# Six of the eight neighbourhood-attention gate units of an encoder layer, computed as three pairs with seven block products each

## The chip, the cores and the metric

The kernel runs on one core of one Trainium2 chip. The core has five engines that work through their own queues in order and wait for one another by semaphores: PE (TensorE, the matmul engine; its weight loads are listed apart as PEld), DVE (VectorE), ACT (ScalarE), POOL (GpSimd) and SP (SyncE), which here only issues transfers. Sixteen DMA engines carry out the transfers. The metric is the time of one execution in microseconds (us), the median of several runs; lower is better. Beside it there is one profiled execution, which is the source of all durations.

## The reference, cut to what matters

The layer takes 512 tokens of width 1024. It projects them to queries, keys, values and gate logits for three attention branches, merges the gated branches, normalises, and ends with 16 expert feed-forward blocks that pick their tokens.

```python
z = jnp.einsum('bsd,df->bsf', x, w_in[l])
q_na, k_na, v_na, q_g, k_g, v_g, q_m, gate_logits = jnp.split(z, _split_points(), axis=-1)
y_na  = neighbourhood_attention(...)      # branch 0
y_gqa = gqa_attention(...)                # branch 1
y_mem = memory_attention(...)             # branch 2
branches = jnp.stack([y_na, y_gqa, y_mem], axis=2)
proj = jnp.einsum('bsgk,gkd->bsgd', branches, w_branch[l])
gates = jax.nn.sigmoid(gate_logits + b_gate[l]).reshape(B, S, N_BRANCH, D)
merged = jnp.sum(gates * proj, axis=2)
mix = jnp.einsum('bsd,de->bse', merged, w_out[l])
x = layer_norm(DN_ALPHA * x + mix, ln1_g[l], ln1_b[l])
ffn = expert_choice_ffn(x, w_router[l], w_gate_up[l], w_down[l])   # 16 experts
x = layer_norm(DN_ALPHA * x + ffn, ln2_g[l], ln2_b[l])
```

The change is in the gate logits of branch 0: for each of eight groups of 128 gate columns, a product of a 1024 x 128 piece of the weights with the 512 tokens, then the sigmoid, which the kernel writes as a tanh of half the argument.

## The kernel before, in words

**Units.** The dense weights arrive as 74 units of 128 x 1024 numbers (512 KB each), in the order in which PE uses them. Units 34 to 53 belong to the neighbourhood queries and keys and to branch 1; 54 to 61 are the eight gate units of branch 0; 62 to 65 are its projections (two projection products each, `pr0` to `pr7`); 66 to 73 are the output projection (`wo`, `woc`). `Stream` handles them: `_dma` (L162) issues a unit's transfer on SP into one of two halves of the tile `raw_twin` (the first units go to wide tiles), `_split` (L176) turns a unit into a rounded high part (a copy on ACT, L100) and a low part (a subtraction on DVE, L101), `take` hands it out and `prefetch` keeps splits and transfers two units ahead. A unit's transfer can be issued only when the unit two before it in `raw_twin` has been split. The split parts live in three homes that rotate.

**Products.** Each product is done three times, high by high, high by low and low by high, into the same PSUM bank (`t_piece`, L281, matmuls at L284 to L286). A gate unit is thus 8 x 3 = 24 matmuls of 128 x 128 weights with 512 columns. The tokens are `xh` and `xl`. A run of 256-column matmuls of the same kind stands in `n_chunk` (L307 and its neighbours, tile `gq`).

**Order.** The program's order on each engine is the order written out in the code. `run` (L805) walks through a stage; at each `yield` it takes a step of the attention pipeline (`at.step()`) and one piece of background work from the list `bg`. Branch 1 (`g_branch(1)`) has 22 yields, six in each of its first three rounds; the gate stage of branch 0 (`g_na_gates`, L568) has one per unit. After it comes `g_na_proj` (L964), which for each projection product multiplies by the gate (L973), adds the merged sum (L974) and splits the result for the output projection (L979, L986), all of it on DVE and ACT. The router's weight scaling, its sums on PE (`wps`, L935) and its centring (L938, L939) are background pieces in the gate stage. PSUM has eight banks: three rotate under the name `mm`, two each under `S` and `T`, one under `Y`.

**Expert blocks.** 201 MB of expert weights come in blocks of 1 or 2 MB (`w<-in_wx`, issued at L843). `RING` lists the tiles (Q1 to Q7, raw, Q9, VS, G1, M) in the order in which blocks go to them; each of these tiles has an earlier use, and a block waits until that is over. `ring.more(n)` loads the next block if fewer than n are in. It is hooked into the issue of units 60, 62, 64 and 66 (the list `after`), then 71 and 73; `ring.upto(9)` follows in the output projection. The rest waits for Q9, which holds the split parts of the last output-projection units, and from there on the blocks stream.

**Tiles that the change touches.** Q4 holds the query parts of branch 1, then twice the position bias `bm` of even head pairs, then the gates `sg`. Q1 holds the neighbourhood queries and keys, Q2 the output of branch 1, Q6 its keys, Q7 the attention's probabilities (`att_twin`), VS the shifted values. From the last attention step on, Q1, Q2, Q5, Q6, Q7 and VS have no use but the ring's.

Of the kernel before, what the change touches and what calls it, by code (L numbers as in the profile page):

```python
# [9 lines left out]
F32 = mybir.dt.float32  # L10
# [8 lines left out]
P = 128  # L19
# [53 lines left out]
def layer_kernel(ctx: ExitStack, tc: tile.TileContext, xt, xn, first0, wu, bgate, rpb, gains, wrt,  # L73
# [14 lines left out]
    def R(tag, shape, name, dt=F32, bufs=None):  # L88
        return rp.tile(shape, dt, name=name, tag=tag, bufs=bufs)
# [3 lines left out]
    def PB(tag, name, shape=(P, 512)):  # L93
        return ps.tile(list(shape), F32, name=name, tag=tag, bufs=PS_BUFS[tag])
# [4 lines left out]
    def hi_lo(hi, lo, src):  # L99
        nc.scalar.copy(hi, src)  # L100
        nc.vector.tensor_tensor(lo, src, hi.bitcast(F32), op=ALU.subtract)  # L101
# [398 lines left out]
    def gate_piece(g, j, dst):  # L500
        u, = ws.take()
        ws.prefetch()
        acc = PB("mm", f"gate{g}{j}")
        t_unit(acc, u, xh, xl)
        return lambda: nc.scalar.activation(dst, acc, AF.Tanh, bias=bg_t[:, g * 8 + j:g * 8 + j + 1], scale=0.5)
# [8 lines left out]
    def g_branch(g, first, pre=None):  # L514
        if first:
            ST["macc"] = R("M", [P, KD, S], "macc")
        macc = ST["macc"]
        for jp in range(4):
            th = []
            for jj in range(2):  # L520
                t = R("t", [P, S], f"th{g}{jp}{jj}", bufs=2)
                th.append(t)
                ev = gate_piece(g, 2 * jp + jj, t)
                yield
                ev()
            u, = ws.take()
            ws.prefetch()
            for jj in range(2):
                j = 2 * jp + jj
                acc = proj_piece(u, jj, *ST[f"y{g}"], f"pr{g}{j}")  # L530
                yield
                if first:
                    nc.vector.scalar_tensor_tensor(macc[:, j], th[jj], 1.0, acc, op0=ALU.add, op1=ALU.mult)
                else:
                    tmp = R("tmp", [P, S], f"tm{g}{j}", bufs=2)
                    nc.vector.scalar_tensor_tensor(tmp, th[jj], 1.0, acc, op0=ALU.add, op1=ALU.mult)
                    nc.gpsimd.tensor_tensor(macc[:, j], macc[:, j], tmp, op=ALU.add)
            if pre:
                yield from pre(jp)

    def g_na_qk(hp):
# [4 lines left out]
        for i in range(2):  # L546
# [5 lines left out]
            for h in range(2):  # L552
# [8 lines left out]
                else:  # L561
# [3 lines left out]
                    for o in (hb, lb):  # L565
                        nc.vector.tensor_tensor(klo[o:o + 64, h], src, k[o:o + 64].bitcast(F32), op=ALU.subtract)

    def g_na_gates():  # L568
        sg = R("Q4", [P, KD, S], "sg")
        ST["sg"] = sg  # L570
        for j in range(8):
            ev = gate_piece(0, j, sg[:, j])
            yield
            ev()


    def recip_norm(pt, sm, heads):
# [102 lines left out]
    def na_bias(hp):  # L680
        bf = R("bf", [P, 2, 8, 48], f"bf{hp}")
        for bq in range(2):
            for c in range(8):
                p0 = bq * 64 + c
                nc.sync.dma_start(bf[p0:p0 + 57:8], bass.AP(
                    tensor=rpb.tensor, offset=rpb.offset + 2 * hp * 8 * 63 + 15 - 8 * bq - c,
                    ap=[[64 * 63, 8], [63, 16], [1, 48]]))
        if hp % 2 == 0:
            bm = R("Q4", [P, 2, 3, 256], f"bm{hp}")
# [79 lines left out]
    class Attn:  # L769
# [4 lines left out]
        def add(self, us):  # L774
            self.units += us
# [142 lines left out]
    ones_f = wtmp[:, 2:4].rearrange("p a b -> p (a b)")  # L918
    nc.gpsimd.memset(ones_f, 1.0)
# [12 lines left out]

    def router_sums():
        wps.append(PB("mm", "wps")[:, :2 * NEXP])
        nc.tensor.matmul(wps[0], ones_f, wsum.rearrange("p a e -> p (a e)"), start=True, stop=True)  # L935

    def router_centre():
        nc.vector.tensor_copy(rb, wps[0][:, NEXP:])  # L938
        nc.vector.scalar_tensor_tensor(wg_t, wps[0][:, None, :NEXP].to_broadcast([P, KD, NEXP]), -1.0 / D, wg_t,  # L939
                                       op0=ALU.mult, op1=ALU.add)  # L940
# [55 lines left out]
    def load_x1(h):  # L996
        nc.sync.dma_start(X1[:, 2 * h:2 * h + 2], xn[:, 2 * h:2 * h + 2])
# [886 lines left out]
```

## Time and profile before

| | us |
|---|---|
| median of 3 runs (lowest to highest) | 960.11 (959.11 to 963.5) |
| the profiled execution | 959.47 |
| its span, first to last instruction | 957.7 |
| PE busy | 941.6 (98%) |
| PEld, DVE, ACT, POOL busy | 607.4, 449.9, 277.1, 97.8 |
| gate units of branch 0 on PE (first to last matmul, with attention steps between the first two) | 375.8 to 423.0 |
| projections of branch 0 on PE | 423.0 to 444.8 |
| start of the stream of expert blocks | 499.9 |

How to read it: PE's busy time is modelled from pipelined matmuls, whose records overlap; the distance from one matmul's start to the next is the better measure of its cost. In the rows of groups, the line and the operation are followed by the tile written and the tile read, the shape, the number of instructions, their busy time in us, the mean of one in ns, and the idle time of the engine before them with what ended most of it. In a timeline each row is a start, a duration, engine, line and operation, with the idle time before it in brackets. Times in the text are us from the start of the span.

### The profile page before, as it was taken

What the parts mean: (1) busy time and instruction counts of PE and PEld (TensorE: products, weight loads), DVE (VectorE), ACT (ScalarE), POOL (GpSimd) and SP (SyncE); (2) the same over time, 40 slices, a digit from 0 to 9 for tenths busy, and PEclk for the clock granted to TensorE, in tenths of its full rate; (3) what the DMA queues carried; (4) which work ended last, traced back from release to release, by engine and by line L of the source; (5) the groups of instructions that cost most, each with busy time, mean ns of one, the idle gap of its engine ahead of it and who ended that gap; (6) DMA issues with size and microseconds to landing.
All of it is one profiled execution on the core that took longest, in us unless ns stands there. A gap on an engine that the chain in (4) does not pass through costs nothing.

```text
span 957.7 us, 12975 instructions
## 1 busy us (share of the span) xinstructions
PE 941.6 (98%) x5258; PEld 607.4 (63%) x5258; DVE 449.9 (47%) x855; ACT 277.1 (29%) x545; POOL 97.8 (10%) x112
## 2 busy tenths in 40 slices
PE   9999999999999999999999999999999999999997
PEld 9899878887888888888886333433334333533335
DVE  6347668764366567237464121653222313331426
ACT  6334453543344454233232111100011000100123
POOL 0002303000122231000023004000000000000004
PEclk9999999999999999999999999999999999999999
DMA  9322221211433322566929999999999999999993
GB/s 361 115 67 67 66 67 44 67 49 63 116 87 110 102 83 66 203 253 256 384 74 382 427 425 422 427 431 430 430 430 431 429 430 432 428 433 429 430 423 119
DMA packets 40807, 251.18 MB, mean 262 GB/s; under 512 B 13198, under 2 KB 13582, under 8 KB 25516
## 3 DMA queue, kind: packets, MB, share of 16 engines
q1 hardware_dynamic: 40604, 250.10, 64.9%
q8 instruction: 41, 0.67, 0.3%
q10 hardware_dynamic: 144, 0.26, 0.1%
q14 instruction: 18, 0.15, 0.0%
HBM read 247.46 MB, written 2.10 MB: 261 GB/s over the span
## 4 chain that ended last, share of the span: by engine, by line
PE 89%; DMA 4%; DVE 4%; POOL 1%; ACT 1%; issue 1%; DVEq 0%; ACTq 0%; POOLq 0%
PE g L1322 11%; PE u L1322 10%; PE y L1358 10%; PE gate L284 4%; PE gate L286 4%; PE gate L285 4%; DMA w<-in_wx 4%; PE pr L284 2%; PE pr L285 2%; PE pr L286 2%; PE gy L672 2%; PE ga L1282 2%; PE cb L1455 2%; PE nqk L286 2%; PE nqk L285 2%; PE nqk L284 2%
## 5 line engine op out<-in xcount | busy, mean ns | idle before, releaser
L1322 PE MATMUL g<-w,xs 128*64 128x512 f32 x508 | 134.0, 606 | 1.9 <-DMA w<-in_wx 1.8
L1322 PE MATMUL u<-w,xs 128*64 128x512 f32 x508 | 130.5, 592 | 0.0
L1358 PE MATMUL y<-w,hT 128*64 128x512 f32 x480 | 106.4, 594 | 2.1 <-DMA w<-in_wx 1.4
L1322 PEld LDWEIGHTS u<-w,xs 128*64 128x64 f32 x508 | 36.5, 137 | 72.6 <-issue 71.7
L101 DVE TENSOR_TENSOR los<-raw_twin,whi 128x1024 fp32r<-128x1024 f32 x42 | 52.6, 1252 | 57.6 <-ACT whi L100 57.4
L101 DVE TENSOR_TENSOR y<-y,y 64x512 fp32r<-64x512 f32 x28 | 19.3, 689 | 128.1 <-ACT y L100 128.1
L100 ACT CAST y<-y 64x512 fp32r<-64x512 f32 x28 | 16.2, 579 | 215.6 <-PE y L1358 205.1
L1358 PEld LDWEIGHTS y<-w,hT 128*64 128x64 f32 x480 | 34.0, 137 | 70.2 <-issue 65.3
L286 PE MATMUL gate<-xh,los 128*128 128x512 f32 x192 | 74.8, 390 | 0.0
L1322 PEld LDWEIGHTS g<-w,xs 128*64 128x64 f32 x508 | 30.5, 136 | 52.1 <-issue 44.5
L284 PE MATMUL gate<-xh,whi 128*128 128x512 f32 x144 | 57.2, 397 | 0.0
L285 PE MATMUL gate<-xl,whi 128*128 128x512 f32 x144 | 56.1, 390 | 0.0
L1458 DVE TENSOR_TENSOR acc<-acc,cb 128x512 f32<-128x512 f32 x56 | 35.6, 683 | 37.9 <-PE cb L1456 37.9
L100 ACT CAST whi<-raw_twin 128x1024 fp32r<-128x1024 f32 x42 | 44.1, 1050 | 9.3 <-PE wo L1120 6.2
L1539 POOL TENSOR_TENSOR acc<-acc,ln2g 128x512 f32<-128x512 f32 x8 | 10.0, 1270 | 352.9 <-ACT y L100 352.5
L286 PEld LDWEIGHTS gate<-xh,los 128*128 128x128 f32 x192 | 36.0, 188 | 7.7
L648 ACT ACTIVATE att_twin<-gs,nm 128x512 f32<-128x512 f32 x32 | 21.7, 683 | 49.9 <-DVE nm L647 49.9
L1332 ACT ACTIVATE tg<-g 128x512 f32<-128x512 f32 x16 | 9.5, 596 | 88.9 <-PE g L1322 88.9
L101 DVE TENSOR_TENSOR los<-raw_twin,los 128x1024 fp32r<-128x1024 f32 x20 | 25.0, 1248 | 19.9 <-ACT los L100 19.8
L284 PEld LDWEIGHTS gate<-xh,whi 128*128 128x128 f32 x144 | 27.0, 188 | 6.5 <-issue 1.2
L1345 DVE COPY hT<-ht 128x512 f32<-128x512 f32 x15 | 10.4, 690 | 42.9 <-PE ht L1340 42.8
L285 PEld LDWEIGHTS gate<-xl,whi 128*128 128x128 f32 x144 | 27.1, 188 | 5.4
(460 smaller groups left out, 1880.6 us busy)
## 6 DMA issues: line engine op xcount, KB each, us to landing
w<-in_wx SPq DMA_DIRECT2D x74, 2048.0 KB
w<-in_wx SPq DMA_DIRECT2D x43, 1024.0 KB
raw_twin<-in_wu SPq DMA_DIRECT2D x65, 512.0 KB
raw<-in_wu SPq DMA_DIRECT2D x8, 512.0 KB
xr<-in_xt SPq DMA_DIRECT2D x4, 512.0 KB
macc<-in_xn SPq DMA_DIRECT2D x2, 1024.0 KB
out<-acc SPq DMA_DIRECT2D x7, 256.0 KB
first<-in_first SPq DMA_DIRECT2D x4, 384.0 KB
```

Of the source, the lines that this page charges most:

```text
L100: nc.scalar.copy(hi, src)
L101: nc.vector.tensor_tensor(lo, src, hi.bitcast(F32), op=ALU.subtract)
L284: nc.tensor.matmul(acc, w_h, rh[:, k], start=(k == 0), stop=False)
L285: nc.tensor.matmul(acc, w_h, rl[:, k], start=False, stop=False)
L286: nc.tensor.matmul(acc, w_l, rh[:, k], start=False, stop=(k == nk - 1))
L648: nc.scalar.activation(self.p[:, h], self.s[h], AF.Exp, bias=nm[:, h:h + 1], accum_out=self.sm[:, h:h + 1])
L672: nc.tensor.matmul(self.y[h * 64:h * 64 + 64, :P], ST["vg"][:, kc, kvh * 64:kvh * 64 + 64], self.pt[:, h, kc], start=(kc == 0), stop=(kc = ...
L1282: nc.tensor.matmul(g, XH[:, m, c], oh[:, m, sl], start=(m == 0), stop=False)
L1322: nc.tensor.matmul(GU[e][b][hf * 64:hf * 64 + 64], xs, w[b][hf] if isinstance(w[b], list) else w[b][:, hf * 512:hf * 512 + 512], start=(k ...
L1358: nc.tensor.matmul(y[o * 64:o * 64 + 64], hT[:, c, hf * 64:hf * 64 + 64], w[j][:, o * 512:(o + 1) * 512], start=(k == 0 and j == 0), stop= ...
L1455: nc.tensor.matmul(cb, g[:, m], yh[:, c], start=True, stop=False)
L1458: nc.vector.tensor_tensor(a, a, cb, op=ALU.add)
```

## The change

Gate units 54 and 55 stay as they are. Units 56 to 61 are done as three pairs. For a pair, the weights are a matrix of 1024 rows and 256 columns and the tokens one of 1024 rows and 512 columns; both are cut in two in each direction, and the eight block products become seven products on sums of blocks (`gate_pair`): p1, p6, p5, p2, p7, p3, p4, each of 12 matmuls with 256 columns. The sums of token blocks are made once: twelve background steps on DVE during branch 1 (`token_sums`), and two more splits at the start of the gate stage (`rest`). The sums of weight blocks are made for each pair: four adds on POOL (`GatePair.sums`), then splits on ACT and DVE (`split`); of the pair's second unit only half is split as it is (`second`). The seven results are added on DVE from PSUM to the gates, and the tanh then runs from SBUF. The work for the next pair is interleaved with the products of a pair through the five hooks `nxt`.

The tiles are given out anew: Q4 becomes one tile for the bias, two token sums, weight sums and the gates; Q6 and Q2 take the token sums' split parts, Q1 the weight sums' split parts, VS weight sums, and units 58 to 61 arrive in Q7. `RING` is put in another order, and blocks are loaded at other places: one before unit 62, then those into Q7, Q6, Q1 and Q2 during and right behind the third pair with units 64 and 65 between them. The router's scaling comes behind the last pair's fifth product, its sums and centring into the projections.

```diff
-RING = (("Q2", 2), ("Q1", 2), ("Q5", 2), ("Q7", 2), ("Q4", 2), ("Q3", 2), ("Q6", 2), ("raw", 1), ("Q9", 2), ("VS", 1),
+G0 = 54
+RING = (("Q5", 2), ("Q7", 2), ("Q6", 2), ("Q1", 2), ("Q2", 2), ("Q3", 2), ("Q4", 2), ("raw", 1), ("Q9", 2), ("VS", 1),
         ("G1", 2), ("M", 2))
...
+            elif G0 + 4 <= i < G0 + 8:
+                if i == G0 + 4:
+                    self.wide = R("Q7", [P, 4, 1024], f"raw{i}")
+                t = self.wide[:, i - G0 - 4]
...
+    def token_sums():
...
+        steps = [first, op(s0, s0, l(0, 1), ALU.add), op(s0, s0, l(0, 0), ALU.subtract),
+                 op(s1, h(1, 1), s0, ALU.subtract), lambda: split(1, s0), op(s1, s1, l(1, 1), ALU.add),
+                 op(s0, h(1, 0), s1, ALU.subtract), lambda: split(2, s1), op(s0, s0, l(1, 0), ALU.add),
+                 op(s1, h(1, 1), h(0, 1), ALU.subtract), op(s1, s1, l(1, 1), ALU.add), op(s1, s1, l(0, 1), ALU.subtract)]
+
+        def rest():
+            room("Q2", (3, 4))
+            split(3, s1)
+            split(4, s0)
...
+        def sums(self):
+            q = [r[:, c:c + 512] for r in self.room for c in (0, 512)]
+            (a11, a12), (a21, a22) = ((r[:, :512], r[:, 512:]) for r in self.raw)
+            g = nc.gpsimd.tensor_tensor
+            g(q[0], a21, a22, op=ALU.add)
+            g(q[1], q[0], a11, op=ALU.subtract)
+            g(q[2], a11, a21, op=ALU.subtract)
+            g(q[3], a12, q[1], op=ALU.subtract)
...
+    def block_product(acc, w, t):
+        wh, wl = (x.rearrange("p (k c) -> p k c", k=4) for x in w)
+        for k in range(4):
+            nc.tensor.matmul(acc, wh[:, k], t[0][:, k], start=(k == 0), stop=False)
+            nc.tensor.matmul(acc, wh[:, k], t[1][:, k], start=False, stop=False)
+            nc.tensor.matmul(acc, wl[:, k], t[0][:, k], start=False, stop=(k == 3))
...
+        nxt[0]()
+        block_product(p[1], w.half(w.a1, 0), B[0, 0])
+        nc.scalar.copy(u[:, 0], p[1])
+        block_product(p[6], w.s_part(1), TB[2])
+        add(u[:, 1], u[:, 0], p[6])
+        nxt[1]()
+        block_product(p[5], w.s_part(0), TB[1])
+        add(v[:, 0], u[:, 1], p[5])
+        block_product(p[2], w.half(w.a1, 1), B[1, 0])
+        add(sg[:, j, lo], u[:, 0], p[2])
+        block_product(p[7], w.s_part(2), TB[3])
+        add(sg[:, j + 1, hi], v[:, 0], p[7])
+        add(v[:, 1], u[:, 1], p[7])
+        nxt[2]()
+        yield
+        block_product(p[3], w.s_part(3), B[1, 1])
+        add(sg[:, j, hi], v[:, 0], p[3])
+        tanh(j)
+        nxt[3]()
+        block_product(p[4], w.half(w.a2, 1), TB[4])
+        add(sg[:, j + 1, lo], v[:, 1], p[4])
+        tanh(j + 1)
+        nxt[4]()
+        yield
...
     def g_na_gates():
-        sg = R("Q4", [P, KD, S], "sg")
+        sg = ST["q4"].rearrange("p a (b s) -> p (a b) s", s=S)
         ST["sg"] = sg
-        for j in range(8):
-            ev = gate_piece(0, j, sg[:, j])
+        rest()
+        parts = R("Q1", [P, 4, 1024], "wsum", F32R)
...
+        for i in range(6):
+            if i == 4:
+                ring.more(1)
+            ws._dma()
...
+        for j in (2, 4, 6):
+            ws.used += 2
+            if j < 6:
+                n = GatePair(G0 + j + 2, parts, rooms[j])
+                
+                def ahead():
+                    n.split(0, 2)
+                    n.split(2)
+                nxt = (n.sums, n.first, ahead, lambda: n.split(3), n.second)
+            else:
+                ring.more(2)
+
+                def ahead():
+                    ring.more(3)
+                    ws._dma()
+                nxt = (lambda: None, ws._split, ahead, lambda: ring.more(4), lambda: ws.prefetch(2))
+            yield from gate_pair(w, j, sg, nxt)
+            w = n
...
-    for i in range(4):
-        after[N_UNITS - 14 + 2 * i] = [lambda: ring.more(4)]
+    after[G0 + 11] = [lambda: ring.more(5)]
...
+    token_steps, rest = token_sums()
+    bg.extend(token_steps)
     run(g_branch(1, False, between), 0.5)
...
-    bg.extend([lambda: None, router_scale, lambda: None, router_sums, router_centre])
+    bg.extend([lambda: None] * 6 + [router_scale, lambda: None, router_sums, router_centre])
     run(g_na_gates(), 1.0)
...
-    for i, f in enumerate((lambda: load_x1(0), lambda: load_x1(1), lambda: ring.more(5), load_tri, lambda: ring.more(6))):
+    for i, f in enumerate((lambda: load_x1(0), lambda: load_x1(1), lambda: ring.more(6), load_tri, lambda: ring.more(7))):
```

More of the change, by code (lines that the diff above doesn't have):

```diff
@@ L566, in g_na_qk, with x_block, op, room @@
                         nc.vector.tensor_tensor(klo[o:o + 64, h], src, k[o:o + 64].bitcast(F32), op=ALU.subtract)
+    def x_block(x, k, t):
+        return x[:, 4 * k:4 * k + 4, 256 * t:256 * t + 256]
+    TB = {}
+    def token_sums():
+        q4 = ST["q4"]
+        f = lambda x: x.bitcast(F32)
+        s0, s1 = (q4[:, n].rearrange("p (k c) -> p k c", k=4) for n in (2, 3))
+        h, l = (lambda k, t: f(x_block(xh, k, t))), (lambda k, t: f(x_block(xl, k, t)))
+        def op(dst, a, b, o):
+            return lambda: nc.vector.tensor_tensor(dst, a, b, op=o)
+        def room(tag, ns):
+            t = R(tag, [P, 4, 1024], f"t{ns[0]}", F32R).rearrange("p n (k c) -> p n k c", k=4)
+            for i, n in enumerate(ns):
+                TB[n] = (t[:, 2 * i], t[:, 2 * i + 1])
+        def split(n, src):
+            hi_lo(*TB[n], src)
+        def first():
+            room("Q6", (1, 2))
+            op(s0, h(0, 1), h(0, 0), ALU.subtract)()
+        steps = [first, op(s0, s0, l(0, 1), ALU.add), op(s0, s0, l(0, 0), ALU.subtract),
[6 more added lines that the diff above has]
+            split(4, s0)
+        return steps, rest
@@ new lines, in layer_kernel, with __init__, first, split @@
+    class GatePair:
+        def __init__(self, i, parts, room):
+            self.i, self.parts = i, parts
+            self.s = parts[:, 0:2], parts[:, 2:4]
+            self.room = room
+            self.raw = [ws.raw[i], ws.raw[i + 1]]
+        def sums(self):
[6 more added lines that the diff above has]
+            g(q[3], a12, q[1], op=ALU.subtract)
+        def first(self):
+            ws._split()
+            self.a1 = ws.hl.pop(self.i)
+        def split(self, lo, hi=None):
+            part = lambda x: x.rearrange("p a n -> p (a n)")[:, 512 * lo:512 * (hi or lo + 1)]
+            raw = self.room[lo // 2][:, 512 * (lo % 2):512 * (lo % 2) + 512 * ((hi or lo + 1) - lo)]
+            hi_lo(part(self.s[0]), part(self.s[1]), raw)
+        def second(self):
+            raw = ws.raw.pop(self.i + 1)
+            self.a2 = home(self.i + 1)
+            hi_lo(self.a2[0][:, 512:], self.a2[1][:, 512:], raw[:, 512:])
+            ws.ns += 1
+        def s_part(self, n):
+            return tuple(x[:, n // 2, (n % 2) * 512:(n % 2) * 512 + 512] for x in self.s)
+        def half(self, u, h):
+            return tuple(x[:, h * 512:h * 512 + 512] for x in u)
@@ L568, in g_na_gates @@
     def g_na_gates():
-        sg = R("Q4", [P, KD, S], "sg")
+        sg = ST["q4"].rearrange("p a (b s) -> p (a b) s", s=S)
         ST["sg"] = sg
-        for j in range(8):
-            ev = gate_piece(0, j, sg[:, j])
-            yield
-            ev()
+        rest()
+        parts = R("Q1", [P, 4, 1024], "wsum", F32R)
+        q4 = ST["q4"]
+        w = GatePair(G0 + 2, parts, (q4[:, 2], q4[:, 3]))
+        for j in range(2):
+            u, = ws.take()
+            if j == 0:
+                w.first()
+                w.sums()
+            else:
+                w.split(0, 2)
+            acc = PB("mm", f"gate0{j}")
+            t_unit(acc, u, xh, xl)
+            yield
+            nc.scalar.activation(sg[:, j], acc, AF.Tanh, bias=bg_t[:, j:j + 1], scale=0.5)
@@ new lines, in g_na_gates @@
+        w.split(2)
+        w.split(3)
+        w.second()
+        for i in range(6):
+            if i == 4:
+                ring.more(1)
+            ws._dma()
+        both = R("VS", [P, 2, 1024], "wsumraw")
+        rooms = {2: (both[:, 0], both[:, 1]), 4: (both[:, 0], q4[:, 3])}
+        for j in (2, 4, 6):
[6 more added lines that the diff above has]
+                nxt = (n.sums, n.first, ahead, lambda: n.split(3), n.second)
+            else:
+                ring.more(2)
[5 more added lines that the diff above has]
+            w = n
```

18 lines of the change are left out of this document (14 added, 4 removed).

## The prediction

> **What bounds the kernel now.** I read the page first (busy shares, chain), then stretches of the span with each engine's busy time, then the SyncE queue's waits.
>
> ```profile
> span 957.7 us, 12975 instructions
> PE 941.6 (98%) x5258; PEld 607.4 (63%) x5258; DVE 449.9 (47%) x855; ACT 277.1 (29%) x545; POOL 97.8 (10%) x112
> PE 89%; DMA 4%; DVE 4%; POOL 1%; ACT 1%; issue 1%; DVEq 0%; ACTq 0%; POOLq 0%
> ...
> 296.00:330.00 34.00, 34.00 (x189) 28.39 (x188) 21.86 (x36) 15.57 (x33) 7.70 (x8) 1.00 0.31 92
> 396.00:410.00 14.00, 14.00 (x64) 11.60 (x63) 3.96 (x5) 4.63 (x6) 0.00 (x0) 1.00 0.84 323
> 423.30:445.00 21.70, 21.70 (x97) 17.98 (x96) 17.21 (x24) 8.81 (x12) 0.00 (x0) 1.00 0.48 186
> 482.00:500.00 18.00, 18.00 (x126) 16.48 (x125) 11.38 (x50) 6.62 (x15) 3.65 (x14) 1.00 0.01 5
> 500.00:930.00 430.00, 424.18 (x2187) 169.49 (x2185) 137.43 (x274) 55.05 (x99) 21.40 (x20) 1.00 1.00 425
> ...
> SPq L843 <- PE woc L1119: 24.2, 1, 24.2
> 499.93 64.86 SPq L843 DMA_DIRECT2D w<-in_wx  x21
> ```
>
> In a stretch row stand length, busy time of PE, PEld, DVE, ACT and POOL (instructions), granted clock, DMA share and GB/s. The chain is TensorE (PE) for 89%. Through the gates and projections PE is packed, so a microsecond taken out there or put in there arrives at the end. From 500 us on, the expert weights stream at 425 GB/s with the DMA engines full; that stream doesn't cancel a shift ahead of it, because it starts (499.93) when SyncE's wait for the last output-projection matmul ends, and the DMA share before it is 0.01. So what counts is when PE leaves the gate and projection stages. VectorE (DVE) is 17.21 of 21.70 us busy in the projections (423 to 445): there it has little room.
>
> **The change: what PE saves.**
>
> ```profile
> 52.06 0.28 PE L306 MATMUL gq<-whi,xh 128*128 128x256 f32 x1
> 57.81 1.03 PE L590 MATMUL ms<-mkvzs,qmT 128*128 128x256 f32 x4
> 389.45 0.61 PE L761 MATMUL ny<-att_twin,ropevg 128*64 128x128 f32 x8
> 389.99 0.50 PE L284 MATMUL gate<-xh,whi 128*128 128x512 f32 x1
> 401.00 0.30 PE L935 MATMUL wps<-wtmp 128*128 128x32 f32 x2
> 401.14 0.48 PE L284 MATMUL gate<-xh,los 128*128 128x512 f32 x1
> 423.03 0.39 PE L284 MATMUL pr<-yn,whi 128*128 128x512 f32 x1
> ```
>
> Six gate units (144 matmuls of 512 columns) take 389.99 to 423.03, 33.04 us, 0.14 of it the router's wps: 0.2285 per matmul. They become three pairs of seven products of twelve 256-column matmuls, 252 in all. The price of those is the gq run: 48 back to back from 52.06 to 57.81, 0.1198 each, and the border between two of its chunks of 24 costs nothing. 252 x 0.1198 = 30.19 us. wps moves into the projections with its 0.14. Saved: 33.04 - 0.14 - 30.19 = 2.71 us. The number of columns falls by an eighth (21504 for 24576), but each matmul keeps some 13 ns beside its columns, and there are 108 more of them.
>
> The Trainium skill, page "TensorE: Matmul & The Clock Gate", section "Back-to-back issue gap", gives sustained spacings of 81 ns at 128 columns and 131 ns at 512, with weight load and stream both setting them. By these, 144 x 131 = 18.9 us would become 252 times something between (20.4 to 33.0): a loss. The rows here (228 and 120 ns) disagree, so I don't use them.
>
> **Costs beside PE.** Durations:
>
> ```profile
> L101 DVE TENSOR_TENSOR los<-raw_twin,whi 128x1024 fp32r<-128x1024 f32 x42 | 52.6, 1252 | 57.6 <-ACT whi L100 57.4
> L100 ACT CAST whi<-raw_twin 128x1024 fp32r<-128x1024 f32 x42 | 44.1, 1050 | 9.3 <-PE wo L1120 6.2
> L101 DVE TENSOR_TENSOR yn<-ny,yn 128x256 fp32r<-128x256 f32 x8 | 3.4, 422 | 8.6 <-ACT yn L100 8.6
> L475 ACT COPY mkvzs<-gq 128x256 f32<-128x256 f32 x8 | 3.0, 380 | 1.9 <-PE gq L308 1.9
> L748 ACT COPY att_twin<-nt 128x512 f32<-128x512 f32 x8 | 4.6, 575 | 11.2 <-PE nt L743 11.2
> L505 ACT ACTIVATE sg<-gate,consts 128x512 f32<-128x512 f32 x8 | 5.5, 691 | 23.1 <-PE gate L286 23.1
> ...
> 375.01 1.28 POOL L537 TENSOR_TENSOR macc<-macc,tm 128x512 f32<-128x512 f32 x1 [17.18 <-DVE tm L536]
> 381.04 2.19 POOL L537 TENSOR_TENSOR macc<-macc,tm 128x512 f32<-128x512 f32 x1 [4.75 <-DVE tm L536]
> 380.88 1.22 DVE L101 TENSOR_TENSOR los<-raw_twin,whi 128x1024 fp32r<-128x1024 f32 x1
> 404.00 0.17 DVE L938 COPY lnT<-wps 128x16 f32<-128x16 f32 x1
> 404.08 0.28 DVE L939 SCALAR_TENSOR_TENSOR wr_t<-wps,wr_t 128x128 f32<-128x128 f32 x1
> 426.02 0.69 DVE L973 SCALAR_TENSOR_TENSOR tm<-sg,pr 128x512 f32<-128x512 f32 x1 [5.35 <-PE pr L286]
> 426.74 0.69 DVE L974 TENSOR_TENSOR tm<-tm,macc 128x512 f32<-128x512 f32 x1
> 430.07 0.68 DVE L986 SCALAR_TENSOR_TENSOR ml<-tm,mh 128x512 fp32r<-128x512 f32 x1
> ...
> 0.72 1.81 SPq L231 DMA_DIRECT2D first<-in_first  x4
> 4.15 0.83 ACT L100 CAST firsth<-first 128x768 fp32r<-128x768 f32 x1 [2.16 <-DMA first<-in_first]
> 9.10 1.05 ACT L100 CAST whi<-raw_twin 128x1024 fp32r<-128x1024 f32 x1 [0.41 <-DMA raw_twin<-in_wu]
> 10.34 1.05 ACT L100 CAST los<-raw 128x1024 fp32r<-128x1024 f32 x1 [0.20 <-DMA raw<-in_wu]
> ```
>
> *Token sums in branch 1.* Twelve steps: ten DVE operations and two splits, 12 x 1.25 = 15.0 us on DVE and 2.1 on ACT, over twelve yields, two of the branch's rounds of some 34 us (the row 296 to 330 is one), each with 12 us of DVE free. I cost them at nothing; uncovered, they would cost PE up to 15.0. The other two token splits (2.5 us of DVE) open the gate stage under two plain gate units, 24 matmuls of 0.2285 each.
>
> *First pair.* PE reaches it at 389.99 as now. Its weight sums are four POOL adds: 1.28 each, 2.19 where a DVE split with two SBUF inputs runs beside one (375.01 against 381.04; the split keeps its 1.22). Behind the macc add of 381.04, now under four splits in a row, they begin near 386.0; the second is done at 388.6, cast 389.6, low part 390.8. Product p6 asks for it at 391.4: no wait, by 0.6.
>
> The Trainium skill, page "SBUF — State Buffer", section "Who interferes with whom", has the later of the two block until the first is done. In these rows only POOL's time grows; if DVE blocked as well, each split could lose up to one add, 1.28 us.
>
> *Second pair.* Units 58 to 61 now go to Q7, free only after the last attention matmul (389.45 + 0.61). A first transfer landed 3.4 us after its issue (0.72 to 4.15), the next units 1.25 apart (9.10, 10.34): 58 at 393.9, 59 at 395.1. Two adds, one beside a split: 398.9; cast and low part: 401.1. p6 of the second pair asks at 401.5: next to no wait (I allow 0.15); each us later is a us lost.
>
> *What the second pair leaves behind.* DVE and ACT work in order, and the fourth sum's split stands behind a tanh that stands behind an add. In queue order: half split of unit 59 done 407.1 (add of p3 403.0, tanh and fourth sum's split 404.8, add of p4 405.2, tanh, cast, low part); split of 60, 409.0; four adds, 410.5; three sums, 412.3; add of p3, 412.7; tanh, cast, low part of the fourth sum, 414.5; add of p4, 414.9; tanh, cast and low part of half unit 61, 416.8. PE isn't held (the third pair runs 410.1 to 420.3), but Q7 is read until 416.8.
>
> *The weight blocks on SyncE's queue.* Now they go one each behind units 60, 62, 64 and 66. After: Q5 before unit 62; then in the third pair Q7, Q6, unit 64, Q1, unit 65, Q2, in order, Q7 waiting for 416.8. A block of 2 MB takes 2.097 MB / 425 GB/s = 4.93 us; the offset from issue to landing is 3.4 less the first transfer's own 0.9, 2.5. Unit 64 lands at 416.8 + 2.5 + 4.93 + 4.93 + 1.25 = 430.4. Its split stands in DVE's queue right behind the first projection's evacuation (426.6). DVE waits: cast 431.5, low part 432.7, and behind it the moved router centring (0.45, done 433.1), which holds the PSUM buffer that projection 3 needs (three rotate, and wps takes a turn between projections 0 and 1). A projection is 12 matmuls, 2.73 us; PE wants that buffer at 420.3 + 0.14 + 3 x 2.73 = 428.6: **4.5 us lost**. DVE then has 2 x (0.69 + 0.69 + 0.68) + 1.22 = 5.3 us of work per 5.45 of PE and doesn't catch up; unit 66, behind Q1 and Q2, lands near 442.8, so the last evacuation ends at 450.8, where the third output-projection sum wants its buffer at 449.5: **1.3 us lost**. Bounds of the two together: 0 if unit 64 is in time, and 13.2, worked the same way, if the DMA gives the 323 GB/s of the row 396 to 410 (6.5 us a block); I take 5.8, by the 425 of the long row.
>
> *At nothing:* the router scaling (four short DVE operations, under 1.3 us) delays two adds of the third pair that PE doesn't wait for; uncovered 1.3. The new order of tags leaves the order of the expert blocks as it is, and nine blocks are in before the stream in both; uncovered, a block is 4.93. The POOL memsets now wait for the pairs' tiles, with nothing urgent behind.
>
> **Sum.** -2.71 + 0.15 + 4.5 + 1.3 = +3.2 us. The profiled execution took 959.47 (span 957.7 and 1.8 around it); 962.7 for it. The median, 960.11, is 0.64 above that: 963.3.
>
> **Rivals.**
> 1. *The units aren't late*, because the second pair's tail is shorter or the DMA serves unit 64 beside the blocks. The 2.71 stays: 957.4. For it: Q7's release rests on a chain of a dozen small steps, and 4 us less of it is enough. Against: the two blocks alone take 9.9 us.
> 2. *Other side: the blocks come slower.* Same place, unit 64 at projection 3 and unit 66 at the output projection. At 6.5 us a block the losses are 13.2 and 0.4 in the pairs: +10.9, 971.0. It decides (+4.8) from about 5.3 us a block. For it: 323 GB/s at 396 to 410. Against: that row has gaps (share 0.84).
> 3. *Transfers share the rings instead of queueing:* 58 and 59 then land with 60, 61 and Q5, 4.2 MB, at 402.5; p6 gets its sums at 407.4, 5.9 late; unit 64 isn't late: 960.11 - 2.7 + 5.9 = 963.3. Against: the starting units landed 1.25 apart, in order.
> 4. *256-column matmuls held by their weight loads:* 252 loads of 0.19,
>
> ```profile
> L307 PEld LDWEIGHTS gq<-los,xh x96: 188/192/192, 52.1 to 104.5; 128*128 128x128 f32 x96
> ```
>
>    47.9 us for 33.0, +15, 975. The gq run had such a load every 0.120 us, so it is all but excluded. [...]
>
> **How the numbers follow.** Forecast 0.48, rival 1 0.22, rival 2 0.19, rival 3 0.05, rival 4 0.02, a gain beyond the products' own 0.04. 0.5% (4.8 us) is about what can be told from no change: faster means below 955.3, only the last case, 0.04; slower means above 964.9, rivals 2 and 4 and the forecast's upper end, 0.27; within, 0.69. The likeliest case's own range is 961.0 to 965.3; the whole range, 957.2 to 966.5, takes in rivals 1 and 3 and the near part of rival 2 and leaves out somewhat under 0.2.
>
> **What would show it.** 84 matmuls of a pair in 10.1 us and no PE wait at the seams of pairs; the block into Q7 issued near 417; ACT idle for unit 64's transfer until about 430; a gap on PE of 3 to 5 us before projection 3, with DVE (router centring) as releaser, and one over 1 us before the output projection's third sum; after 452 everything as before, shifted. The prediction is wrong if unit 64's cast waits for no transfer, if PE waits inside the pairs, or if PE waits during the token sums in branch 1.

## The result, and the profile after

The changed kernel takes 966.94 us (median of 6 runs, 965.84 to 969.28); the kernel before took 960.33 beside it (median of 6). The ratio is 1.0070, with a 95% interval of 1.0051 to 1.0089: 6.6 us slower, where 3.2 were forecast. The profiled execution took 967.82 us. The page of the changed kernel, its first lines and the shares of the chain:

```profile
span 966.0 us, 13284 instructions
PE 942.6 (98%) x5366; PEld 612.6 (63%) x5366; DVE 483.2 (50%) x899; ACT 286.7 (30%) x561; POOL 126.2 (13%) x124
PE 82%; DMA 8%; DVE 5%; ACT 2%; issue 2%; POOL 2%; DVEq 0%; ACTq 0%; POOLq 0%; SPq 0%
```

PE's share of the chain falls from 89 to 82% and DMA's doubles to 8%: somewhere the end now hangs on a transfer. The stretches of the changed kernel show where (length, busy time of PE, PEld, DVE, ACT and POOL, granted clock, that is the share of full speed that PE was given, DMA share, GB/s); they are a round of branch 1, the pairs, the projections and the expert stream:

```profile
296.00:330.00 34.00, 34.00 (x188) 28.42 (x187) 29.54 (x44) 18.02 (x37) 10.86 (x8) 1.00 0.30 90
390.30:421.40 31.10, 30.51 (x254) 30.31 (x253) 22.22 (x36) 14.45 (x23) 15.06 (x11) 1.00 0.48 188
421.40:452.80 31.40, 25.00 (x100) 20.04 (x99) 20.27 (x33) 10.48 (x14) 0.41 (x4) 0.89 0.80 334
508.00:938.00 430.00, 423.86 (x2187) 169.40 (x2185) 137.48 (x274) 55.15 (x99) 21.41 (x20) 1.00 1.00 425
```

In branch 1 DVE has 29.54 us of work for 21.86 before, and PE is still busy for all 34.00. The pairs take 31.1 us where six units took 33.0. The projections take 31.4 where they took 21.8, with 6.4 us of PE idle and, beside it, a granted clock of 0.89. The expert stream is as before.

The waits of PE in that part of the changed kernel, and then its timeline around the long one (start, duration, engine, line, operation, and in brackets the idle time before and what ended it):

```profile
PE pr L289 <- DVE wr_t L1101: 6.4, 1, 6.4
PE gp L653 <- DVE wsum L102: 0.6, 1, 0.6
```

```profile
418.54 0.80 SPq L1004 DMA_DIRECT2D w<-in_wx  x2
419.92 0.33 SPq L175 DMA_DIRECT2D raw_twin<-in_wu  x1
...
429.75 0.39 PE L291 MATMUL pr<-yn,los 128*128 128x512 f32 x1
433.81 1.04 ACT L101 CAST los<-raw_twin 128x1024 fp32r<-128x1024 f32 x1 [8.68 <-DMA raw_twin<-in_wu]
434.89 1.22 DVE L102 TENSOR_TENSOR los<-raw_twin,los 128x1024 fp32r<-128x1024 f32 x1 [7.17 <-ACT los L101]
436.12 0.28 DVE L1101 SCALAR_TENSOR_TENSOR wr_t<-wps,wr_t 128x128 f32<-128x128 f32 x1
436.55 0.77 PE L289 MATMUL pr<-yn,whi 128*128 128x512 f32 x1 [6.40 <-DVE wr_t L1101]
437.11 0.63 PE L290 MATMUL pr<-yn,whi 128*128 128x512 f32 x1
437.54 0.63 PE L291 MATMUL pr<-yn,los 128*128 128x512 f32 x1
```

This is the forecast chain, link by link: the blocks into Q7 and Q6, unit 64 behind them, its cast, its low part, the router centring, projection 3. But behind the wait the matmuls last 0.63 us for 0.39 and stand 0.43 apart for 0.23. The granted clock in three stretches around it:

```profile
428.00:436.00 8.00, 2.14 (x10) 1.41 (x8) 1.11 (x1) 1.58 (x2) 0.00 (x0) 0.95 1.00 424
436.50:442.00 5.50, 5.46 (x13) 4.33 (x14) 4.95 (x7) 2.21 (x3) 0.00 (x0) 0.50 1.04 442
442.00:452.00 10.00, 10.00 (x46) 8.28 (x45) 8.77 (x14) 4.03 (x6) 0.00 (x0) 1.00 0.44 167
```

The clock is halved (0.50) for the 5.5 us behind the wait, so projection 3 takes 5.25 us instead of 2.72. The projections lose 9.63 us in all: 6.57 by the wait (from start to start, less one normal spacing), 2.67 by the slow clock, 0.14 by the router's sums and 0.25 in small gaps. It isn't this execution alone: the mean granted clock is 0.993 or 0.994 in all six runs, and 0.996 to 0.998 in the runs of the kernel before that stand beside the experiments. The wait forecast before the third output-projection sum isn't there.

The table gives the three stages of every kernel that was run: from the first matmul of the pairs (of the third gate unit, before) to projection 0, from there to the output projection, from there to the start of the expert stream, where the wait for the last output-projection matmul ends. Each number is the difference of two starts in the kernel's profiled execution.

| kernel | pairs | projections | to the stream | sum |
|---|---|---|---|---|
| before | 33.04 | 21.76 | 55.14 | 109.94 |
| changed | 31.17 | 31.39 | 55.15 | 117.71 |
| e1_busy | 31.37 | 28.57 | 56.44 | 116.38 |
| e9_part | 30.97 | 28.04 | 56.42 | 115.43 |
| e2_bank | 31.05 | 28.82 | 55.67 | 115.54 |
| e3_one | 30.97 | 27.84 | 56.75 | 115.56 |
| e4_units | 31.00 | 22.14 | 56.39 | 109.53 |
| e5_spread | 31.12 | 22.11 | 55.16 | 108.39 |
| e6_early | 30.33 | 22.86 | 55.15 | 108.34 |
| e7_noadd | 30.33 | 26.59 | 55.29 | 112.21 |
| e8_both | 30.33 | 22.06 | 55.20 | 107.59 |

By these sums the changed kernel loses 7.8 us in its profiled execution. The two profiled executions differ by 8.35 us and the medians by 6.6, because the changed kernel's lies 0.9 above its median and that of before 0.9 below.

### The profile page after: what moved, and what is told of

Same layout as the page of the kernel before. It is cut to its first block, busy times and chain, and to the rows that moved or that the text cites. A ratio compares the mean times of both kernels' runs of the same rounds, so it can differ in the third digit from the quotient of the medians.

```text
span 966.0 us, 13284 instructions
## 1 busy us (share of the span) xinstructions
PE 942.6 (98%) x5366; PEld 612.6 (63%) x5366; DVE 483.2 (50%) x899; ACT 286.7 (30%) x561; POOL 126.2 (13%) x124
## 4 chain that ended last, share of the span: by engine, by line
PE 82%; DMA 8%; DVE 5%; ACT 2%; issue 2%; POOL 2%; DVEq 0%; ACTq 0%; POOLq 0%; SPq 0%
PE g L1484 11%; PE u L1484 10%; PE y L1520 9%; DMA w<-in_wx 6%; PE gate L289 3%; PE gate L291 3%; PE gate L290 3%; PE pr L289 2%; PE pr L290 2%; PE pr L291 2%; PE gy L831 2%; PE ga L1444 2%; PE cb L1617 2%; PE nqk L290 2%; PE nqk L291 2%
## 5 line engine op out<-in xcount | busy, mean ns | idle before, releaser
L102 DVE TENSOR_TENSOR los<-raw_twin,whi 128x1024 fp32r<-128x1024 f32 (+1 forms) x40 | 50.9, 1273 | 41.5 <-ACT whi L101 41.4
L291 PE MATMUL gate<-xh,los 128*128 128x512 f32 x144 | 56.1, 390 | 0.0
L101 ACT CAST whi<-raw_twin 128x1024 fp32r<-128x1024 f32 (+1 forms) x40 | 41.6, 1040 | 12.7 <-PE wo L1282 6.5
L289 PE MATMUL gate<-xh,whi 128*128 128x512 f32 x112 | 44.6, 399 | 0.0
L290 PE MATMUL gate<-xl,whi 128*128 128x512 f32 x112 | 43.7, 390 | 0.0
L102 DVE TENSOR_TENSOR los<-raw_twin,los 128x1024 fp32r<-128x1024 f32 x18 | 22.5, 1252 | 21.8 <-ACT los L101 21.6
L291 PEld LDWEIGHTS gate<-xh,los 128*128 128x128 f32 x144 | 27.0, 188 | 5.8
L542 POOL TENSOR_TENSOR macc<-macc,tm 128x512 f32<-128x512 f32 x8 | 18.5, 2310 | 78.3 <-DVE tm L541 78.3
L889 ACT ACTIVATE att_twin<-att_twin,nm 128x256 f32<-128x256 f32 x32 | 16.1, 503 | 38.9 <-DVE nm L887 38.9
```

Of the source, the lines that this page charges most:

```text
L289: nc.tensor.matmul(acc, w_h, rh[:, k], start=(k == 0), stop=False)
L290: nc.tensor.matmul(acc, w_h, rl[:, k], start=False, stop=False)
L291: nc.tensor.matmul(acc, w_l, rh[:, k], start=False, stop=(k == nk - 1))
```

## The experiments

Theory: unit 64 is late because its transfer stands behind two blocks, and the wait costs its own length and then a stretch of halved clock. Rivals: the router's moved place makes the wait; PE waits for DVE's backlog and not for a transfer; the transfers share the DMA rings instead of being served in the order of issue; the slow matmuls have a cause other than the idle time.

### PE kept busy through the wait: e1_busy and e9_part

```diff
+                if j == 3:
+                    keep = PB("Y", "keep")
+                    for _ in range(24):
+                        nc.tensor.matmul(keep[:, :P], ident, ident, start=True, stop=True)
                 acc = proj_piece(u, jj, *ST["y0"], f"pr0{j}")
```

e9_part has 19 in place of 24.

> The changed kernel with 24 small matmuls (identity by identity, 128 columns, result unused) put on PE between projections 2 and 3, where it now stands idle for 6.4 us. They should take 24 x 0.227 = 5.4 us, so they end before projection 3 can start. Theory (the idle time itself costs a second time, because the granted clock is halved behind it): projection 3 still starts near 436.5 us, as unit 64 is as late as before, but its 12 matmuls stand 0.227 apart instead of 0.427, 2.4 to 2.7 us less: 964.3. Rival (the slow matmuls come from something else in that stretch, such as the transfers at 430 GB/s or DVE reading PSUM): spacing stays 0.427 and the time 966.9. If the small matmuls delay projection 3, the time is above 967.

> The kernel with small matmuls in PE's wait, but 19 instead of 24, so that some 2.0 us of the wait stay empty. The runs so far: 0.8 and 1.3 us of idle time left the clock full, 2.7 halved it for some 3.4 us. Theory (a fixed length of idle time between 1.3 and 2.7 decides): the spacing behind is either 0.227 in all of projection 3, or 0.427 in at least seven of its matmuls. Rival (it depends on where the idle time lies against a window that runs on its own): either can come, and this single run can't tell it from the first if the clock falls.

e1_busy took 965.75 us, ratio 1.0057 (1.0042 to 1.0072), 1.2 less than the changed kernel. In its stretches the first is the filled wait and the second projection 3:

```profile
430.00:436.80 6.80, 6.09 (x52) 5.78 (x50) 1.54 (x4) 1.58 (x2) 0.00 (x0) 1.00 0.99 415
436.90:439.70 2.80, 2.79 (x12) 2.34 (x13) 2.63 (x5) 0.63 (x1) 0.00 (x0) 1.00 1.06 446
```

The DMA engines are as full as in the changed kernel (0.99 and 1.06), DVE is busy in the same way, and the clock is 1.00: twelve matmuls in 2.8 us. So neither transfers nor DVE slowed them; the idle time did. The size was missed by half: 2.4 us were won in projection 3, and 1.1 came back at another place. The waits of PE in e1_busy:

```profile
PE wo L1284 <- DVE tm L1139: 1.0, 1, 1.0
PE pr L289 <- DVE wr_t L1101: 0.8, 1, 0.8
```

The first line is the wait before the third output-projection sum that the prediction had, at 1.3. In the changed kernel the slow matmuls of projection 3 gave DVE the time to catch up. That e1_busy, at full clock, has the wait again fits this. In e9_part the clock stayed full too (964.32 us, one run), but only 1.4 us of the wait were left empty where 2.0 were meant, so it says little more than the 1.3 us seen before.

### The router's sums in another bank: e2_bank

```diff
-        wps.append(PB("mm", "wps")[:, :2 * NEXP])
+        wps.append(PB("T", "wps")[:, :2 * NEXP])
```

> The changed kernel with the router's sums in a PSUM bank of another name (T, unused here) instead of one of the three banks of the projections; unit 64 stays late. Theory (unit 64 is late, and the router's place only decides which projection feels it): projection 3 starts at 430.0 without a wait and PE stands instead before projection 4, which needs unit 64 itself and the bank of projection 1, until about 437.0: 4.3 us instead of 6.6. If a wait of that length halves the clock too, 966.9 - 2.4 = 964.5; if it doesn't, 962.0. Rival (the moved router centring alone makes the wait): the wait goes altogether, 957.7. Rival (the bank has no part in it): 966.9.

The runs gave 965.2, 965.2 and 968.6 us, ratio 1.0068 (1.0042 to 1.0095; a fourth run, of 4966.3 us, is left out). The runs can't be told from those of the changed kernel; by the trace the stages are 2.2 us shorter than in the changed kernel, near the 2.4 expected with a falling clock. Projection 3 starts at 429.64 without a wait, and PE waits before projection 4. Its wait, then the stretches of that wait and of projection 4:

```profile
PE pr L289 <- DVE tm L1135: 3.6, 1, 3.6
```

```profile
432.50:436.00 3.50, 0.03 (x1) 0.00 (x0) 2.09 (x4) 1.57 (x2) 0.00 (x0) 0.92 0.96 411
436.20:441.40 5.20, 5.20 (x12) 4.05 (x13) 4.54 (x7) 2.21 (x3) 0.00 (x0) 0.50 1.05 447
```

So the bank decides which projection feels the late unit, and 2.8 us of the wait with it; it doesn't make the wait. And the clock is halved behind 3.6 us of idle time as behind 6.4.

### One block behind unit 64: e3_one

```diff
-                    ring.more(3)
                     ws._dma()
+                    ring.more(3)
```

> The changed kernel with one of the two weight blocks (that into Q6) issued behind unit 64 instead of ahead of it; everything behind stands in the same order. Theory (transfers are served in the order of issue, 2.1 MB at about 425 GB/s): unit 64 lands 4.9 us earlier, near 428.9, its cast ends at 429.9, low part and centring at 431.6; projection 3 waits 1.7 us instead of 6.6, too short for the clock to fall; unit 65 lands when it did (439.7) and projection 6 now waits some 2 us for it. 966.9 - 4.9 - 2.6 + 2.1 = 961.5. Rival (transfers share the rings): unit 64 lands where it did, 966.9. Rival (PE waits for DVE's backlog and not for the transfer): 966.9 as well, with unit 64 landed earlier and its cast no earlier.

It took 966.12 us, ratio 1.0061 (1.0045 to 1.0077): the time that the rivals gave, but not for their reasons, as the trace shows. Unit 64 and unit 65 in e3_one (this execution starts its pairs 2.3 us later than the changed kernel's, 1.7 of it from a stretch near 125 us that is shown below):

```profile
420.66 0.33 SPq L1004 DMA_DIRECT2D w<-in_wx  x1
...
429.97 1.05 ACT L101 CAST los<-raw_twin 128x1024 fp32r<-128x1024 f32 x1 [2.71 <-DMA raw_twin<-in_wu]
441.38 1.04 ACT L101 CAST whi<-raw_twin 128x1024 fp32r<-128x1024 f32 x1 [6.83 <-DMA raw_twin<-in_wu]
```

```profile
PE pr L289 <- DVE tm L1135: 3.3, 1, 3.3
PE wo L1280 <- DVE tm L1135: 1.3, 1, 1.3
PE pr L289 <- DVE wr_t L1101: 0.5, 1, 0.5
```

From the issue of the block into Q7 to the cast of unit 64 it is 9.3 us with one block ahead, and 15.3, 15.1 and 14.6 with two (changed kernel, e1_busy, e2_bank). So a block ahead costs the unit 5.3 to 6.0 us: it is the order of issue that counts, and the unit doesn't land where it did, as it would with shared rings. The cast, on ACT, waits for the transfer, so it isn't a backlog of DVE. Projection 3 waits 0.5 instead of 6.4. What was wrong was the rest of my sum: projection 6 now waits 3.3 for unit 65, that wait halves the clock again (1.5 us), and the wait before the third output-projection sum is back. One late unit was exchanged for the next.

The stretch near 125 us bears on the clock. Every kernel here has a wait of PE of 1.8 us there, for POOL; its end in the changed kernel, and then in e3_one with matmuls behind it:

```profile
121.60 0.66 PE L431 MATMUL rT<-ident,ropevg 128*128 128x128 f32 x4 [1.79 <-POOL ropevg L425]
```

```profile
122.34 0.66 PE L431 MATMUL rT<-ident,ropevg 128*128 128x128 f32 x4 [1.84 <-POOL ropevg L425]
...
123.76 0.63 PE L289 MATMUL pr<-ym,los 128*128 128x512 f32 x1
124.18 0.63 PE L290 MATMUL pr<-ym,los 128*128 128x512 f32 x1
```

In e3_one the granted clock is 0.50 from 123.2 to 126.7, which costs 1.7 us; in the other ten profiled executions it stays at 1.00 behind the same wait. So the length of a wait alone doesn't decide whether the clock falls.

### The units ahead of the blocks: e4_units and e5_spread

```diff
-                ring.more(2)
-
                 def ahead():
-                    ring.more(3)
                     ws._dma()
-                nxt = (lambda: None, ws._split, ahead, lambda: ring.more(4), lambda: ws.prefetch(2))
+                    ring.more(2)
+                nxt = (lambda: None, ws._split, ahead, lambda: None, lambda: ws.prefetch(2))
...
-    after[G0 + 11] = [lambda: ring.more(5)]
+    for i in range(3):
+        after[G0 + 11 + i] = [lambda i=i: ring.more(3 + i)]
```

In e5_spread the last two lines are `for i in range(2)` and `after[G0 + 12 + 2 * i]`.

> The changed kernel with unit 64 issued ahead of all blocks of the third pair and one block issued behind each of units 64, 65, 66 and 67 (before: two ahead of unit 64, one ahead of unit 65, one behind it). Theory: no PE wait in the projections at all, the clock full, the projections 21.9 us as before (21.8 and 0.14 for the router's sums), the expert stream from 500 us on only shifted: the saving in the pair stage is left alone, 966.9 - 6.6 - 2.7 = 957.6, 1.6 to 2.9 us under the kernel before. Rival (DVE has too little room in the projections with the split of unit 64 and the centring at its normal time): a PE wait of 1 to 3 us stays, 959 to 961. Rival (the blocks, now later, hold up the start of the expert stream): a new wait behind 500 us, above 961.

> Like the kernel with the units ahead of the blocks, but one block behind every second unit (64, 66, 68) instead of every one, the rest later, where the queue is empty. Theory (one unit and one 2 MB block take 6.1 us of transfer for 5.45 us of PE, so units 65 to 67 still came 1.0 to 1.8 us late and left the last evacuations 0.9 us late before the output projection): the casts of units 65 to 67 wait for no transfer, the wait before the third output-projection sum goes, and from the first product of the pairs to the start of the expert stream the kernel takes some 108.5 us, for 109.94 before, 117.71 in the changed kernel and 109.53 with one block per unit: 960.2 - 1.4 = 958.8. Rival (DVE's own work, 17 of 22 us and now a split and the centring more, is what is late): the wait stays at 0.9 and the time near 960. Rival (the expert stream is limited by the DMA engines and doesn't pass on a gain of 1 us): the stream starts earlier and the time stays at 960.

e4_units took 961.17 us, ratio 1.0012 (0.9997 to 1.0027). The wait in the projections and the slow clock are gone (22.14 us), as expected; 0.9 us of wait before the third output-projection sum stay. Its median is 3.6 us above my sum, of which the stages explain that wait alone. Its profiled execution, the longest of ten, lost the rest in the stream. PE waits 6.7 us there for expert blocks, for 1.8 in the kernel before, and this stretch of e4_units has 390 GB/s, where the kernel before and the changed one have 423:

```profile
560.00:620.00 60.00, 60.00 (x332) 24.38 (x328) 19.77 (x39) 7.88 (x14) 9.90 (x8) 1.00 1.01 390
```

Why stays open. The mean granted clock parts the other nine runs: five with 0.997 or 0.998 took 959.4 to 960.6 us, four with 0.995 or 0.996 took 961.8 to 962.8. So in these four the clock is likely to have been halved somewhere for some us; they have no trace that shows where.

e5_spread took 958.44 us, ratio 0.9987 (0.9973 to 1.0001). The casts of units 65 to 67 wait for no transfer, the wait before the output projection is gone, and the sum of the stages is 108.39 where 108.5 were expected. So that wait came from units that land late behind blocks, not from DVE's own load.

### The split moved ahead, and both: e6_early and e8_both

```diff
         add(v[:, 0], u[:, 1], p[5])
+        if len(nxt) > 5:
+            nxt[5]()
...
-                def ahead():
-                    n.split(0, 2)
+                def ahead(n=n, j=j):
+                    if j == 2:
+                        n.split(0, 2)
                     n.split(2)
                 nxt = (n.sums, n.first, ahead, lambda: n.split(3), n.second)
+                if j == 4:
+                    nxt += (lambda: n.split(0, 2),)
```

e8_both has this, the spread blocks and the bank of e2_bank.

> The same and, in the second pair, the split of the first two weight sums of the third pair moved ahead of two adds that PE doesn't wait for. Theory: the 0.6 us that PE waits for these sums (product p6 of the third pair) go, and nothing takes their place: 0.4 to 0.6 us less than without, some 958.3. Rival: the two delayed adds free their PSUM banks later and PE waits as long there: no difference.

> The kernel with spread blocks and the early split, and in addition the router's sums in a PSUM bank of the name T. Theory: the 0.5 to 0.7 us that PE waited there before projection 2 (for the evacuation of projection 0, whose bank it takes because the router's sums took a turn among the three) go: 958.2 - 0.6 = 957.6, ratio 0.9975. Rival: the next thing that is late takes their place (the cast of unit 63, which stands behind the last tanh, or the evacuations before the output projection): no difference.

e6_early took 958.17 us, ratio 0.9981 (0.9973 to 0.9989), which the runs can't tell from e5_spread (958.44 us). Its pairs are 0.8 us shorter, without a wait; but its projections are 0.75 longer, because projection 2 now waits as long for the evacuation of projection 0, whose bank it takes (0.5 us on DVE's line L1139). The gain was there and was given back one stage later; my rival had looked for it inside the pairs. e8_both takes this wait away by the bank: 957.71 us, ratio 0.9975 (0.9965 to 0.9986), 2.6 us faster than the kernel before and 9 faster than the changed one. In the whole stretch it keeps one wait of PE, which is in the kernel before as well, and its stages show PE without a gap up to the output projection:

```profile
PE x1t L1190 <- DVE macc L1207: 0.3, 1, 0.3
```

```profile
390.40:420.80 30.40, 30.40 (x255) 30.37 (x254) 21.52 (x34) 14.45 (x23) 14.91 (x10) 1.00 0.44 174
420.80:442.80 22.00, 22.00 (x100) 18.21 (x99) 19.30 (x33) 9.85 (x13) 0.47 (x4) 1.00 0.84 321
```

### POOL's adds left out: e7_noadd

```diff
+            if self.i > G0 + 2:
+                for t in q:
+                    nc.gpsimd.memset(t, 0.0)
+                return
             g = nc.gpsimd.tensor_tensor
```

> The changed kernel with the eight POOL adds of the second and third pair left out: their four weight sums are set to zero by POOL instead, which reads nothing, so the gates of these pairs are not those of the layer. The splits on DVE are the same in number and size. Theory (a POOL add and a DVE subtraction with two inputs in SBUF hold each other up, whichever comes second): the splits of the second pair's sums, 2.93 us for two (1024 and 512 wide), 1.44 and 1.33 us, take 1.22 + 0.68, 0.68 and 0.68, and the second pair's tail ends earlier, so that the block into Q7 is issued before 417 instead of 418.5. Rival (they are long for a reason of their own, such as the transfers that land at that time): they stay above 1.3.

The splits of the second pair on DVE, in the changed kernel:

```profile
400.00 2.93 DVE L102 TENSOR_TENSOR wsum<-wsumraw,wsum 128x1024 fp32r<-128x1024 f32 x2 [1.48 <-ACT wsum L101]
404.56 1.44 DVE L102 TENSOR_TENSOR wsum<-wsumraw,wsum 128x512 fp32r<-128x512 f32 x1 [1.30 <-ACT wsum L101]
407.63 1.33 DVE L102 TENSOR_TENSOR los<-raw,whi 128x512 fp32r<-128x512 f32 x1 [1.30 <-ACT whi L101]
```

and in e7_noadd:

```profile
398.24 1.82 DVE L102 TENSOR_TENSOR wsum<-wsumraw,wsum 128x1024 fp32r<-128x1024 f32 x2
401.69 0.69 DVE L102 TENSOR_TENSOR wsum<-wsumraw,wsum 128x512 fp32r<-128x512 f32 x1 [1.30 <-ACT wsum L101]
404.01 0.69 DVE L102 TENSOR_TENSOR los<-raw,whi 128x512 fp32r<-128x512 f32 x1 [1.30 <-ACT whi L101]
```

Without an add beside them the four splits take 2.5 us less. The block into Q7 is issued at 414.81 for 418.54, though not all of that is the adds' hold on DVE: the zeroed sums are also ready sooner. Projection 3 then waits 2.7 us and still takes 4.42 us, so the clock was halved, for 3.4 us, behind 2.7 us of idle time. By the trace it fell only at 432.0, 0.3 us after PE had started again. The kernel took 961.42 us in its one run.

## Why the prediction was wrong, point by point

*Saved on PE, 2.71.* Right to 0.14. Without waits the pairs take 30.33 us (e8_both) where 30.19 were worked out; with the router's 0.14 us, which only move, 2.57 are saved. (The 13 ns that each matmul keeps beside its columns are 11 by the prediction's own two spacings, and its column counts are those of one pair; the sum uses neither.) In the changed kernel 0.8 goes into a wait for the sums of the third pair (from start to start; 0.6 in the row of waits), where the prediction had 0.15 for the second; a PE wait inside the pairs was one of its own signs of being wrong.

*Token sums at nothing.* Right: 7.7 us more of DVE in the branch-1 stretch and PE full. From 125 us to the pairs the changed kernel keeps the same distance to the kernel before (0.28 us, there since the first transfers).

*The mechanism: unit 64 behind two blocks, DVE, the centring, projection 3.* Right, with the releaser named. e4_units removes the wait by the order of issue alone.

*Its size, 4.5.* Too small by 2.1, for three reasons. First, "In these rows only POOL's time grows": no, in the pairs DVE was the later of the two and was held up for 2.5 us; Q7 was released 1.7 us later than worked out. The prediction had the rule that would have said so, from the Trainium skill, page "SBUF — State Buffer", section "Who interferes with whom" (the later one blocks until the first is done), and put it aside because the rows of before happened to show the other order of issue. The trace agrees with the rule: in the changed kernel the splits of 0.69 us took up to 1.44, and POOL's adds of 1.28 up to 2.28. How much of the 1.7 us this makes isn't shown, since the sums of e7_noadd are also ready sooner. Second, "4.93 us a block": from the issue of the first block to the cast of unit 64 it took 15.3 us and not 13.6. The rate itself was right (416 to 451 GB/s from 422 us on); too small was what it took beside it, 2.5 us for the way from issue to landing. In these 15.3 us 5.9 MB were moved (at 385 GB/s in the mean), and the two blocks and unit 64 are 4.7: either the block behind unit 64 already took a share, or the landing was noticed late, and no run parts the two. Q7's release and these transfers make unit 64 3.4 us later. Third, PE, held in the pairs, wanted the bank 1.4 us later than worked out, which takes part of it back.

*The step that failed most: a wait was priced at its length.* Nothing in the sum allowed for the granted clock behind a wait; it cost 2.7 us here, 2.4 of which e1_busy took away by keeping PE busy. In the kernel before, the rows of this stage have a clock of 1.00; the one place where its clock falls is the last 4 us of the span (0.50), when PE's work is over. The Trainium skill, page "TensorE: Matmul & The Clock Gate", section "What's actually happening", has it: half the clock after an idle window of some 3.4 us, full again after a busy one. That section wasn't used, though a wait of 4.5 us was forecast. The runs agree with its half clock (0.50), but not with the length: they show it already behind waits of 2.7 us, and once of 1.8.

*The wait before the third output-projection sum, 1.3.* Right as a mechanism, wrong in the sum: it comes at 1.0 to 1.3 us in e1_busy, where the clock stays full, and in e3_one, where a late unit 65 halves it further on. In the changed kernel it doesn't come on top of the slow projection 3, so the projections lost 6.57 + 2.67 where the prediction had 4.5 + 1.3.

*The rivals.* The units not late, 957.4: that is what e8_both (957.71) and, nearly, e5_spread are. Blocks slower, 971.0: in part true. The DMA engines weren't slower, but the two blocks and unit 64 took 1.7 us longer than worked out, half of the 3.4 us. Shared rings: excluded by e3_one. Weight loads as the bound: excluded by 30.33 us for 252 matmuls.

## What to carry to other kernels

Price a wait of PE at its length plus the clock that can fall behind it: waits of up to 1.4 us cost only themselves here, one of 1.8 us cost 1.7 more in one execution of eleven, and those from 2.7 us on cost 1.5 to 2.9 more. Issue what PE needs next ahead of large transfers that have time, and don't put one large block behind every small one if the two together take longer than PE's step. Where a wait goes, look up what was hidden behind it: three of these kernels lost half or all of a gain to the next thing that was late.

## What the runs showed of the hardware that I had not expected

- The granted clock behind idle time of PE: full after 0.8, 1.3 and 1.4 us (e1_busy, e3_one, e9_part), halved after 2.7, 3.3, 3.6 and 6.4 (e7_noadd, e3_one, e2_bank, changed), and after 1.8 us full in ten executions and halved in one. Read in steps of 0.1 us it stays at 0.50 for 3.4 us in e7_noadd and in both places of e3_one, and for twice that, 6.8, in e2_bank and the changed kernel. It falls 2.7 to 3.0 us after the end of PE's last matmul, in the changed kernel 5.1, and so partly inside the wait or, after the short ones, behind it. What sets the moment wasn't settled.
- At half clock a matmul of 512 columns stands 0.427 us from the next, at full clock 0.227.
- A POOL add and a DVE subtraction with two inputs in SBUF hold each other up whichever comes second: the add up to 2.28 us for 1.28, the subtractions up to 1.44 for 0.69.
